# Eleven opening loads on another engine's queue: a two-layer hybrid trunk on one core

## The chip, the cores and the metric

The kernel runs on one core of one Trainium2 chip. The metric is the time of one execution on the device in microseconds (us); the median of three runs stands for a kernel. The engines are named as the profile names them: PE (TensorE, matrix products), DVE (VectorE), ACT (ScalarE), POOL (GpSimd) and SP (SyncE, which here does nothing but start DMA transfers). Each engine executes its own list of instructions in a fixed order, and waits on semaphores for the others.

## The reference

Two layers of a diffusion trunk work on 128 context rows and 1024 latent rows (1152 rows, nine tiles of 128), D_MODEL 1024, in float32. Each layer first computes a modulation from the condition vectors, which scales, shifts and gates everything behind it:

```python
def trunk_layer(x, cond, P, mixer):
    mod = jnp.einsum('bd,de->be', jax.nn.silu(cond), P['w_ada']) + P['b_ada']
    sh1, sc1, gt1, sh2, sc2, gt2 = jnp.split(mod[:, None, :], 6, axis=-1)
    h = rms_norm(x, P['g_pre_mix']) * (1.0 + sc1) + sh1
    o, extra = mixer(h)
    x = x + gt1 * rms_norm(o, P['g_post_mix'])
    h = rms_norm(x, P['g_pre_mlp']) * (1.0 + sc2) + sh2
    ...
```

The mixer projects h to four groups (latent attention, windowed attention, a gated delta-rule scan, a long convolution) and joins them; a squared-ReLU MLP follows. The filters of the long convolution come from a small network of sines over position features, which depends on neither x nor the condition:

```python
    h = jnp.sin(freq[0] * (feats @ P['hy_w1'].astype(F32) + P['hy_b1'].astype(F32)))
    h = jnp.sin(freq[1] * (h @ P['hy_w2'].astype(F32) + P['hy_b2'].astype(F32)))
```

## The kernel before

**What stands at the start.** The kernel first loads constants with `C` (line 198), all from SP: `condraw` (the condition vectors), `ident` (the identity matrix for transposes), `bada0` (the modulation's bias) and `g_pre_mix0`. ACT turns `condraw` into `cst` with a Silu (line 327); every product of the modulation reads `cst`. Two generators then run against one another. `hy_sines` (line 1496) computes the network of sines for both layers at once: it loads `feats` (17 rows of 1152 values) and six small pieces of the tile `hyw` (for each layer `w1` with 17 rows, `w2` with 64 rows, and `pp`; line 1508), runs three products `hy` of 17 rows, a run of DVE operations on the tile `hya`, a sine on ACT (line 1523), and the same again from `w2`. `lead` (line 2051) loads three tiles of x, runs the first part of the modulation, and loads the other six tiles.

**The modulation's first part.** `ada` (line 385) loads 32 tiles `wada` of 256 KB (line 392) and multiplies each into one accumulating tile, as four products side by side. The tiles rotate through two pools, named T (4 buffers) and L (8 buffers), so twelve can be under way; the thirteenth load waits for a product that has read its buffer. Afterwards ACT copies the sum to `adarow` (line 398), PE transposes it (`adat`), and ACT applies it to the transposed x (`h`, line 481), which becomes `hT`, the input of every product of the input projection (`pj`, weights `wa`, loaded by line 251 and split into `wah` and `wal`).

**What sets the order.** Lists of all engines are made ahead of time by a list scheduler that plays the program through with its own estimates of durations. An instruction that moves in the list at the start shifts the estimates of all that follow, and so the order of instructions far behind it may change too. Each transfer of SP or ACT also takes one of eight completion semaphores (DMAHW0 to DMAHW7), and does not start before the transfer that had the same semaphore last has landed.

**Later places that are named below.** The delta-rule scan of each layer needs an inverse, built on POOL (tiles N, written to DRAM and read back as `NaTG`) and finished by products `G` on PE. The scan itself is the products `u` and `dS` with the state `St`. `ht` and `tt` are transposes, and `hc` is a tile that they read. Later parts of the modulation load `wada` through the same line 392.

Of the kernel before, what the change touches and what calls it, by code (L numbers as in the profile page):

```python
# [34 lines left out]
def shape_constants():  # L35
# [21 lines left out]
    def rope_rows(dim):  # L57
        co, si = angles(dim)
        C = np.repeat(co, 2, 1).T
        S = np.repeat(si, 2, 1).T * np.where(np.arange(dim) % 2 == 0, -1.0, 1.0)[:, None]  # L60
        r = 128 // dim
        return np.tile(C, (r, 1)), np.tile(S, (r, 1))
# [4 lines left out]
    C = np.repeat(co, 2, 1)  # L67
    S = np.repeat(si, 2, 1) * np.where(np.arange(32) % 2 == 0, -1.0, 1.0)[None, :]
    c["rope_k"] = np.stack([C, S], 0).reshape(2, 8, 128, 32).transpose(2, 0, 1, 3).astype(f)

    def feats(L):
# [92 lines left out]
class Trunk:  # L164
# [30 lines left out]
    def S(self, shape, name, bufs=2, dt=F32, p=128):  # L195
        return self.psm.tile([p] + list(shape), dt, tag=name, name=self.nm(name), bufs=bufs)

    def C(self, shape, name, src=None):
        t = self.pc.tile([128] + list(shape), F32, tag=name, name=name)
        if src is not None:  # L200
            self.nc.sync.dma_start(out=t, in_=src)
        return t

    def dram(self, shape, name):
# [115 lines left out]
    def consts(self):  # L320

        I, nc = self.I, self.nc

        cond = self.C((8, 2), "condraw", I["cond"])
        self.cst = self.C((8, 32), "cst")
        nc.vector.memset(self.cst, 0.0)
        nc.scalar.activation(out=self.cst[:, :, 0:2], in_=cond, func=AF.Silu)
        self.ident = self.C((128,), "ident", I["ident"])
        self.mhalf = self.C((1,), "mhalf")
        nc.vector.memset(self.mhalf, -0.5)  # L330
        self.mod = [self.C((3, 8, 2, 2), f"mod{l}") for l in range(DEPTH)]
        self.AB = [self.C((2, 8, 2), f"ab{l}") for l in range(DEPTH)]
        self.gvec = {}
        self.bada = [self.C((48,), "bada0", I["b_ada"][0])]
        self.gvec["g_pre_mix", 0] = self.C((8,), "g_pre_mix0", I["g_pre_mix"][0])

    def scratch(self):

# [189 lines left out]
    def rope_rows(self, x, tab, c):  # L528

        nc = self.nc  # L530
        C, S, sh = (self.H(name=n) for n in ("rC", "rS", "rsh"))
        nc.sync.dma_start(out=C, in_=self.I[tab][0][:, c])
        nc.sync.dma_start(out=S, in_=self.I[tab][1][:, c])
        nc.vector.stream_shuffle(out=sh, in_=x[:, c], mask=[i ^ 1 for i in range(32)])
        nc.gpsimd.tensor_tensor(out=sh, in0=sh, in1=S, op=ALU.mult)
        nc.vector.tensor_tensor(out=x[:, c], in0=x[:, c], in1=C, op=ALU.mult)
        nc.vector.tensor_tensor(out=x[:, c], in0=x[:, c], in1=sh, op=ALU.add)
# [958 lines left out]
    def hy_sines(self, tag):  # L1496

        nc, I = self.nc, self.I
        V = nc.vector
        small = self.W(name="hyw", tag=tag)  # L1500
        w1, w2, pp = small[:, 0:128], small[:, 128:256], small[:, 256:260]
        V.memset(w2, 0.0)
        h = self.W(name="feats", tag=tag)
        nc.sync.dma_start(out=h[:17], in_=I["feats"])
        for l in range(DEPTH):
            q = slice(64 * l, 64 * l + 64)
            for dst, src in ((w1[:17, q], I["hy_w1"][l]), (w2[q, q], I["hy_w2"][l]), (pp[q], I["hy_pp"][l])):
                nc.sync.dma_start(out=dst, in_=src)
        for st, w in ((0, w1[:17]), (1, w2)):
            a = self.W(name="hya", tag=tag)  # L1510
            for c0, n in NCH:
                ps = self.P(name="hy")
                self.mm(ps[:, :n], w, h[:w.shape[0], c0:c0 + n])
                V.tensor_scalar(out=a[:, c0:c0 + n], in0=ps[:, :n], scalar1=pp[:, 2 * st:2 * st + 1],
                                scalar2=pp[:, 2 * st + 1:2 * st + 2], op0=ALU.add, op1=ALU.mult)
            k = self.W(name="hyk", tag=tag)
            M = 1.5 * 2 ** 23
            V.tensor_scalar(out=k, in0=a, scalar1=1.0 / (2 * math.pi), scalar2=M, op0=ALU.mult, op1=ALU.add)
            V.tensor_scalar(out=k, in0=k, scalar1=M, scalar2=None, op0=ALU.subtract)
            V.scalar_tensor_tensor(out=a, in0=k, scalar=-6.28125, in1=a, op0=ALU.mult, op1=ALU.add)  # L1520
            V.scalar_tensor_tensor(out=a, in0=k, scalar=-(2 * math.pi - 6.28125), in1=a, op0=ALU.mult, op1=ALU.add)
            V.tensor_scalar(out=a, in0=a, scalar1=3.1415925, scalar2=-3.1415925, op0=ALU.min, op1=ALU.max)
            nc.scalar.activation(out=a, in_=a, func=AF.Sin)
            h = a
            yield 5
        self.sines = h
# [714 lines left out]
```

## Time and profile before

| | us |
|---|---|
| median of three runs | 3825.18 |
| the three runs | 3819.07 to 3829.11 |
| the profiled execution | 3828.84 |
| its span in the trace | 3827.1 |
| PE busy in the span | 3531.1 (92%) |
| DVE busy | 2279.6 (60%) |
| ACT busy | 1355.6 (35%) |

The span is the time from the first to the last instruction of the trace; the remaining 1.7 us of the profiled execution lie around it. Shares are averages over the whole kernel; the stretches of it have different limits, so the windows and the waits are read beside them.

### The profile page before, as it was taken

What the parts mean: (1) busy time and instruction counts of PE and PEld (TensorE: products, weight loads), DVE (VectorE), ACT (ScalarE), POOL (GpSimd) and SP (SyncE); (2) the same over time, 40 slices, a digit from 0 to 9 for tenths busy, and PEclk for the clock granted to TensorE, in tenths of its full rate; (3) what the DMA queues carried; (4) which work ended last, traced back from release to release, by engine and by line L of the source; (5) the groups of instructions that cost most, each with busy time, mean ns of one, the idle gap of its engine ahead of it and who ended that gap; (6) DMA issues with size and microseconds to landing.
All of it is one profiled execution on the core that took longest, in us unless ns stands there. A gap on an engine that the chain in (4) does not pass through costs nothing. (4 is left out here: it accounts for less than half of the span.)

```text
span 3827.1 us, 57478 instructions
## 1 busy us (share of the span) xinstructions
PE 3531.1 (92%) x21710; PEld 2958.8 (77%) x21710; DVE 2279.6 (60%) x4583; ACT 1355.6 (35%) x2970; POOL 853.1 (22%) x806
## 2 busy tenths in 40 slices
PE   7989888899899999999989798787999999999998
PEld 4879764366689999999968797645666899999997
DVE  5765577696645444444586664768884544444446
ACT  5434343264542222122354234323564422222112
POOL 1151521264430000000131524213553200000003
PEclk9999889897899999999999898897889999999999
DMA  5356486831421111111234465756314211111113
GB/s 202 115 120 158 139 275 202 235 90 39 138 87 47 45 44 34 44 45 45 96 103 131 108 144 161 258 187 177 84 50 138 72 45 45 45 45 42 40 41 121
DMA packets 364672, 405.31 MB, mean 106 GB/s; under 512 B 115815, under 2 KB 237157, under 8 KB 364394
## 3 DMA queue, kind: packets, MB, share of 16 engines
q1 hardware_dynamic: 364394, 401.63, 34.9%
q8 instruction: 171, 2.80, 0.3%
q14 instruction: 107, 0.88, 0.1%
HBM read 298.34 MB, written 103.19 MB: 105 GB/s over the span
## 5 line engine op out<-in xcount | busy, mean ns | idle before, releaser
L213 PE MATMUL hid<-hT,w1h 128*128 128x384 f32 x3072 | 786.5, 335 | 0.1
L213 PE MATMUL pj<-hT,wah 128*128 128x384 f32 x2112 | 575.1, 351 | 9.0 <-ACT wah L253 4.2
L1831 DVE TENSOR_TENSOR acc<-acc,mo 128x512 f32<-128x512 f32 x504 | 346.1, 687 | 391.8 <-PE mo L213 391.8
L213 PEld LDWEIGHTS hid<-hT,w1h 128*128 128x128 f32 x3072 | 557.7, 188 | 14.4 <-ACT h L481 1.1
L213 PE MATMUL hid<-hT,w1l 128*128 128x384 f32 x1536 | 514.1, 335 | 0.0
L213 PE MATMUL mo<-w2h,ul 128*128 128x512 f32 x1116 | 435.0, 392 | 0.0
L213 PE MATMUL mo<-w2h,uh 128*128 128x512 f32 x1080 | 422.7, 391 | 0.0
L213 PE MATMUL mo<-w2l,uh 128*128 128x512 f32 x1080 | 422.7, 391 | 0.0
L213 PEld LDWEIGHTS pj<-hT,wah 128*128 128x128 f32 x2112 | 395.3, 196 | 21.9 <-issue 7.8
L662 POOL TENSOR_TENSOR e<-e,e 128x512 f32<-128x512 f32 (+1 forms) x216 | 307.3, 1424 | 313.8 <-DVE el L232 145.2
L269 POOL TENSOR_TENSOR postr<-postr,mhalf 128x1 f32<-128x1 f32 x36 | 22.3, 621 | 1568.9 <-DVE postr L268 1568.6
L213 PE MATMUL pj<-hT,wal 128*128 128x384 f32 x1056 | 367.5, 348 | 0.7 <-DVE wal L232 0.7
L242 ACT CAST w2h<-w 128x512 fp32r<-128x512 f32 x128 | 70.3, 619 | 732.9 <-PE mo L213 728.8
L213 PEld LDWEIGHTS hid<-hT,w1l 128*128 128x128 f32 x1536 | 288.3, 188 | 2.5
L232 DVE TENSOR_TENSOR el<-e,eh 128x512 fp32r<-128x512 f32 (+1 forms) x252 | 241.4, 977 | 25.1 <-ACT eh L653 20.4
L213 PEld LDWEIGHTS mo<-w2h,ul 128*128 128x128 f32 x1116 | 209.6, 188 | 46.1
L213 PEld LDWEIGHTS mo<-w2h,uh 128*128 128x128 f32 x1080 | 202.8, 188 | 37.5
L213 PEld LDWEIGHTS mo<-w2l,uh 128*128 128x128 f32 x1080 | 202.7, 188 | 36.5
L213 PEld LDWEIGHTS pj<-hT,wal 128*128 128x128 f32 x1056 | 206.3, 195 | 4.6 <-issue 2.0
L1814 DVE SCALAR_TENSOR_TENSOR relu<-hid,relu 128x384 f32<-128x384 f32 x180 | 99.5, 554 | 166.9 <-ACT relu L1813 166.9
L213 PE MATMUL ada<-wada,cst 128*32 128x512 f32 x384 | 130.8, 692 | 45.5 <-DMA wada<-in_w_ada 45.4
L232 DVE TENSOR_TENSOR wal<-wa,wah 128x512 fp32r<-128x512 f32 x88 | 67.6, 773 | 147.2 <-ACT wah L253 118.2
(502 smaller groups left out, 6366.6 us busy)
## 6 DMA issues: line engine op xcount, KB each, us to landing
w<-in_w SPq DMA_DIRECT2D x256, 256.0 KB
wada<-in_w_ada SPq DMA_DIRECT2D x192, 256.0 KB
wa<-in_wa SPq DMA_DIRECT2D x88, 256.0 KB
x<-xres SPq DMA_DIRECT2D x21, 512.0 KB
x<-in_x SPq DMA_DIRECT2D x18, 512.0 KB
Q<-rscr SPq DMA_DIRECT2D x32, 288.0 KB
o<-oscr SPq DMA_DIRECT2D x18, 512.0 KB
xres<-x SPq DMA_DIRECT2D x36, 256.0 KB
```

The lines of the kernel that those rows point to most:

```text
L213: self.last = self.nc.tensor.matmul(out, l, r, start=start, stop=stop, skip_group_check=True)
L232: self.nc.vector.tensor_tensor(out=lo, in0=x, in1=hi.bitcast(F32), op=ALU.subtract)
L242: self.nc.scalar.copy(out=hi[:, q], in_=st)
L269: self.nc.gpsimd.tensor_tensor(out=out, in0=out, in1=self.bcs(self.mhalf[:out.shape[0]], out.shape), op=ALU.pow)
L662: self.nc.gpsimd.tensor_tensor(out=acc, in0=acc, in1=e, op=ALU.add)
L1814: nc.vector.scalar_tensor_tensor(out=r[:, :n], in0=ps[:, :n], scalar=0.0, in1=r[:, :n], op0=ALU.max, op1=ALU.mult)
L1831: nc.vector.tensor_tensor(out=acc[t][:, ns], in0=acc[t][:, ns], in1=ps, op=ALU.add)
```

## The change

Four calls of `C` in `consts`, the load of `feats` and the six loads of `hyw` are started by ACT (`nc.scalar`) in place of SP. Nothing is computed differently.

```diff
-    def C(self, shape, name, src=None):
+    def C(self, shape, name, src=None, queue=None):
         t = self.pc.tile([128] + list(shape), F32, tag=name, name=name)
         if src is not None:
-            self.nc.sync.dma_start(out=t, in_=src)
+            (queue or self.nc.sync).dma_start(out=t, in_=src)
         return t
...
-        cond = self.C((8, 2), "condraw", I["cond"])
+        q = nc.scalar
+
+        cond = self.C((8, 2), "condraw", I["cond"], q)
...
-        self.ident = self.C((128,), "ident", I["ident"])
+        self.ident = self.C((128,), "ident", I["ident"], q)
...
-        self.bada = [self.C((48,), "bada0", I["b_ada"][0])]
-        self.gvec["g_pre_mix", 0] = self.C((8,), "g_pre_mix0", I["g_pre_mix"][0])
+        self.bada = [self.C((48,), "bada0", I["b_ada"][0], q)]
+        self.gvec["g_pre_mix", 0] = self.C((8,), "g_pre_mix0", I["g_pre_mix"][0], q)
...
-        nc.sync.dma_start(out=h[:17], in_=I["feats"])
+        nc.scalar.dma_start(out=h[:17], in_=I["feats"])
         for l in range(DEPTH):
             q = slice(64 * l, 64 * l + 64)
             for dst, src in ((w1[:17, q], I["hy_w1"][l]), (w2[q, q], I["hy_w2"][l]), (pp[q], I["hy_pp"][l])):
-                nc.sync.dma_start(out=dst, in_=src)
+                nc.scalar.dma_start(out=dst, in_=src)
```

SP's list before, behind the loads of `condraw`, `ident` and `bada`. A name in brackets is a semaphore for which the instruction waits; DMAHW4, in the row of `wada_180`, is the one that `feats` raises.

```order
L201 DMA g_pre_mix_108<-in_g_pre_mix 128x8
L1504 DMA feats_115<-in_feats 17x1152
L1508 DMA hyw_113<-in_hy_w 17x64
L1508 DMA hyw_113<-in_hy_w 64x64 [waits DVE_49]
L1508 DMA hyw_113<-in_hy_pp 64x4
L1508 DMA hyw_113<-in_hy_w 17x64 [waits DMAHW0_49]
L1508 DMA hyw_113<-in_hy_w 64x64 [waits DMAHW1_49]
L1508 DMA hyw_113<-in_hy_pp 64x4 [waits DMAHW2_49]
L392 DMA wada_177<-in_w_ada 128x512 [waits DMAHW3_49]
L392 DMA wada_180<-in_w_ada 128x512 [waits DMAHW4_49]
L392 DMA wada_183<-in_w_ada 128x512 [waits DMAHW5_49]
```

Seven more `wada` follow there, then three tiles of x, then 18 `wada`. SP's list after the change begins with twelve `wada`; these are the last two of them and what follows. DMAHW1 is raised in turn by `wada_177`, by `feats` and by the second `w1`, and DMAHW7 by `g_pre_mix` and then by the first `pp`.

```order
L393 DMA wada_224<-in_w_ada 128x512 [waits DMAHW4_49]
L393 DMA wada_230<-in_w_ada 128x512 [waits DMAHW6_49]
L1791 DMA x_140<-in_x 128x1024 [waits DMAHW7_49]
L1791 DMA x_152<-in_x 128x1024 [waits DMAHW0_49]
L1791 DMA x_164<-in_x 128x1024 [waits DMAHW1_49]
L393 DMA wada_227<-in_w_ada 128x512 [waits DMAHW2_49,PE_49]
L393 DMA wada_233<-in_w_ada 128x512 [waits DMAHW3_49,PE_49]
```

The eleven small loads are gone from SP, and `wada_227` is the first load that waits for PE (for five products: three `hy` and two `ada`); later the `wa_378` that stood ahead of `wada_287` stands behind the six loads of x. ACT's list, which opened with the table load and the Silu, now opens so:

```order
L201 DMA condraw<-in_cond 128x16
L201 DMA ident<-in_ident 128x128
L201 DMA bada_106<-in_b_ada 128x48
L328 ACT_TABLE_LOAD [waits DMAHW0_49]
L328 ACTIVATE cst<-condraw 128x8x2 [waits DVE_49]
L201 DMA g_pre_mix_108<-in_g_pre_mix 128x8
L1505 DMA feats_115<-in_feats 17x1152 [waits DMAHW1_49]
L1509 DMA hyw_113<-in_hy_w 17x64 [waits DMAHW3_49]
L1509 DMA hyw_113<-in_hy_w 64x64 [waits DMAHW5_49,DVE_49]
L1509 DMA hyw_113<-in_hy_pp 64x4 [waits DMAHW7_49]
L1509 DMA hyw_113<-in_hy_w 17x64 [waits DMAHW1_49]
L1509 DMA hyw_113<-in_hy_w 64x64 [waits DMAHW3_49]
```

Eight of the eleven loads now stand behind the Silu, and the second `w1` (17x64) waits on DMAHW1 until `feats` has landed. PE's list opens in both kernels with the three products `hy` that need `feats` and both `w1`; behind them come ten products `ada` before, thirteen after.

The scheduler also orders later stages anew; this is the second layer's inverse on PE, before, where the first `G` stands behind two of nine transposes of `hc`.

```order
L213 MATMUL pj_19970<-hT_11027,wal_19914 128x384
L229 MATMUL ht_3641_20144<-ident,hc_19588 128x128 x2
L213 MATMUL G_19719<-NaTG_19702,Q_19155 32x32
L213 MATMUL G_19757<-NaTG_19702,Q_19155 32x32
L229 MATMUL ht_3641_20144<-ident,hc_19588 128x128
```

The same place after the change:

```order
L213 MATMUL pj_19970<-hT_11027,wal_19914 128x384
L229 MATMUL ht_3641_20144<-ident,hc_19588 128x128 x4
L229 MATMUL ht_3643_20152<-ident,hc_19588 128x128 x4
L229 MATMUL ht_3645_20160<-ident,hc_19588 128x128
L213 MATMUL G_19719<-NaTG_19702,Q_19155 32x32
```

All nine transposes now stand ahead of the first `G`; and the two `G` that read `Q_19172`, which followed the transposes directly before the change, stand behind 40 products `pj` after it.

## Rows read from the trace of the kernel before

**Rows 1.** The page: engines' busy time, share of the span, instructions; the DMA queue.
```profile
PE 3531.1 (92%) x21710; PEld 2958.8 (77%) x21710; DVE 2279.6 (60%) x4583; ACT 1355.6 (35%) x2970; POOL 853.1 (22%) x806
q1 hardware_dynamic: 364394, 401.63, 34.9%
```
**Rows 2.** Windows: start:end us, length, busy of PE PEld DVE ACT POOL, PEclk, DMA share, GB/s.
```profile
8.00:10.00 2.00, 0.66 (x1) 0.50 (x2) 0.00 (x0) 0.00 (x0) 0.00 (x0) 1.00 0.51 141
10.00:12.00 2.00, 2.00 (x4) 1.00 (x3) 0.68 (x1) 0.00 (x0) 0.00 (x0) 1.00 0.98 346
30.00:38.00 8.00, 7.18 (x22) 1.11 (x20) 2.04 (x3) 2.03 (x3) 0.00 (x0) 1.00 1.06 389
40.00:60.00 20.00, 14.41 (x84) 11.82 (x85) 14.90 (x54) 19.76 (x47) 5.48 (x8) 0.96 0.76 264
80.00:180.00 100.00, 100.00 (x523) 86.48 (x522) 63.57 (x156) 50.03 (x93) 10.93 (x8) 1.00 0.32 112
2400.00:2600.00 200.00, 153.06 (x1396) 99.50 (x1392) 143.21 (x427) 60.42 (x200) 45.90 (x44) 0.86 0.72 235
```
**Rows 3.** Timeline of SP, 0 to 42 us: start, length, line, operation, how many.
```profile
0.74 0.39 SPq L201 DMA_DIRECT2D condraw<-in_cond  x1
...
2.60 0.33 SPq L1504 DMA_DIRECT2D feats<-in_feats  x1
...
6.24 6.38 SPq L392 DMA_DIRECT2D wada<-in_w_ada  x10
...
33.03 0.33 SPq L392 DMA_DIRECT2D wada<-in_w_ada  x1
```
**Rows 4.** What SP waited for in 0 to 14 us: total, times, longest.
```profile
SPq L392 <- DMA feats<-in_feats: 1.6, 1, 1.6
```
**Rows 5.** Timeline of SP, 8 to 10 us.
```profile
8.47 1.77 SPq L392 DMA_DIRECT2D wada<-in_w_ada  x4
```
**Rows 6.** Timeline of ACT, 0 to 42 us; in brackets the idle time before, and its end.
```profile
2.41 1.28 ACT L327 ACT_TABLE_LOAD   x1 [2.41 <-DMA condraw<-in_cond]
3.70 0.22 ACT L327 ACTIVATE cst<-condraw 128x16 f32<-128x16 f32 x1
...
37.64 0.62 ACT L253 CAST wah<-wa 128x512 fp32r<-128x512 f32 x1 [2.15 <-DMA wa<-in_wa]
```
**Rows 7.** Timeline of PE, 0 to 42 us.
```profile
9.34 4.20 PE L213 MATMUL hy<-feats,hyw 17*128 17x384 f32 x6 [9.34 <-DMA hyw<-in_hy_w]
13.47 5.86 PE L213 MATMUL ada<-wada,cst 128*32 128x512 f32 x20
38.26 1.04 PE L213 MATMUL ada<-wada,cst 128*32 128x512 f32 x2 [0.30 <-DMA wada<-in_w_ada]
```
**Rows 8.** Timeline of PE, 2163 to 2182 us (layer 1's inverse).
```profile
2175.34 0.41 PE L213 MATMUL G<-NaTG,Q 32*32 32x32 f32 x4 [8.57 <-DMA NaTG<-nscr]
...
2176.44 1.54 PE L229 MATMUL ht<-ident,hc 128*128 128x128 f32 x6
2180.49 0.39 PE L213 MATMUL G<-NaTG,Q 32*32 32x32 f32 x4 [2.51 <-DMA NaTG<-nscr]
```
**Rows 9.** The page: a group of products, count | busy us, mean ns | idle before.
```profile
L213 PE MATMUL pj<-hT,wah 128*128 128x384 f32 x2112 | 575.1, 351 | 9.0 <-ACT wah L253 4.2
```
**Rows 10.** What PE waited for, 1900 to 2800 us: total, times, longest.
```profile
PE ada L213 <- DMA wada<-in_w_ada: 27.9, 7, 14.5
...
PE u L213 <- DVE St L1368: 8.9, 4, 4.3
```
**Rows 11.** Timeline of POOL, 228 to 285 us (layer 0's inverse), two of its pieces.
```profile
238.59 0.55 POOL L1212 TENSOR_TENSOR N<-N,tmp 72x156 f32<-72x156 f32 x1
239.22 5.04 POOL L1210 TENSOR_TENSOR tmp<-N,U 72x175 f32<-72x175 f32 x1
```
**Rows 12.** What PE waited for, 180 to 720 us (layer 0's mixer).
```profile
PE G L213 <- DMA NaTG<-nscr: 18.3, 1, 18.3
```

## The prediction

> **What bounds the kernel now.** I read the page's shares first, then windows, then the waits of PE and of SP. PE is busy 92% of the span, the DMA queue 34.9% [rows 1]: over the whole kernel PE is the bound. The windows show where it is not [rows 2]. From 80 to 180 us PE is busy 100 of 100 us, and time saved ahead of such a stretch is kept, because PE simply starts it earlier. In the opening it is different. PE starts its first product at 9.34 us, when `hyw` has landed [rows 7]; from 10 us on the DMA engines are full (0.98, then 1.06 at 389 GB/s), while in 8 to 10 us they stand at 0.51 [rows 2]. The last product of the modulation's first part starts at 38.26 and waits for its own load [rows 7]. So the opening is a stream of loads, and what counts is when the stream starts and whether it has holes. From 40 to 60 us ACT is busy 19.76 of 20 us [rows 2]; it applies the modulation there and starts when the modulation is ready, so an earlier end of the stream passes through.
>
> The hole ahead of the stream has two parts. SP issues eleven small loads from 0.74 on and its first `wada` at 6.24 [rows 3]. Its next `wada` needs the semaphore that `feats` raises: SP waited 1.6 us for it [rows 4] and went on at 8.47 [rows 5]. `feats` was issued at 2.60 [rows 3], so from issue to landing it took 8.47 - 2.60 = 5.87 us.
>
> **SP's opening.** SP's first `wada` moves from 6.24 to about 0.74: 5.50 us. The `wa` that stood ahead of `wada_287` now stands behind the x loads: 256 KB at 389 GB/s [rows 2] is 0.67 us. If the stream had no hole, the last product would start 5.50 + 0.67 = 6.2 us sooner. That is one end. But only twelve buffers exist: the thirteenth load, `wada_227`, waits for the second product `ada`, which stands in PE's list behind the three products `hy`. So the stream stops after twelve `wada` and three x, and goes on when PE starts. What decides is when PE starts; I call that T0 (9.34 before).
>
> **ACT's opening and T0.** `condraw` is issued at 0.74 as before, and the table load starts at 2.41 when it lands: 1.67 us from issue to landing. Table load and Silu end at 3.70 + 0.22 = 3.92 [rows 6]. Before, nothing on ACT's list was waiting there; now eight loads stand behind it. `g_pre_mix` takes an issue of about 0.4 (0.39 [rows 3]), so `feats` is issued at 4.3 where it was 2.60. Landing 5.87 later: 10.2. The second `w1` waits for that landing by its semaphore, and needs at least the 1.67 of `condraw`: T0 = 11.9 at the earliest. At the other end `feats` no longer has the DMA engines nearly to itself, as it had before; twelve `wada` run beside it. If that doubles the part behind the fixed 1.67, that is 5.87 - 1.67 = 4.2 us more, T0 = 16.1. No row shows `feats` beside a full stream. I take the middle, T0 = 14.0, because DMA is full as soon as SP streams [rows 2], and the stream covers only part of the time of `feats`.
>
> The Trainium skill, "DMA: Bandwidth & Descriptors", section "Queues, rings and completion order", has each DMA engine take turns between its queues by packet, which speaks against the change: `feats` would share its engine with the weights. By that rule T0 lies nearer the late end. The sum does not use it.
>
> **From T0 to the last product.** The three `hy` take 4.2 us in this trace (six records from 9.34 to 13.54) and the first two `ada` together about 1.4 (1.06 for one, and 5.86/20 = 0.29 for a next, as four run at once) [rows 7]. So `wada_227` is issued at T0 + 5.6. Issue 0.4, 1.67 to landing, then 20 `wada` at 256 KB/389 GB/s = 0.67 and one `wb` of 192 KB at 0.5: T0 + 5.6 + 0.4 + 1.67 + 13.5 + 0.5 = T0 + 21.7. With T0 = 14.0 the last product starts at 35.7 instead of 38.26: **-2.6 us**, ends -4.7 (T0 = 11.9) and -0.5 (T0 = 16.1). The opening breaks even at T0 = 16.6. So PE's first product comes later than before, and the modulation ends sooner all the same.
>
> The sines on ACT (second product `hy`) hide beside the `ada` products; the x tiles are normalised there as well. If that cover is gone, each sine costs what ACT waits for DVE, but none stands on the chain to the last `ada`. The moved `wa` must be cast by ACT behind the modulation: 0.62 us [rows 6], in the stretch where ACT is full [rows 2]: **+0.6**, ends 0 and 0.7.
>
> **The order further on.** Most of the new order changes nothing where PE is full. Where PE waits it may. In layer 0 PE waits 18.3 us for the inverse [rows 12], whose inputs stand 3 to 13 products later in PE's list; at 575.1/2112 = 0.27 us a product [rows 9] that is 0.8 to 3.5 us later for POOL's chain, and the wait grows by it: **+0.8**, since the first input moves by three. That chain can also move by itself: one of POOL's pieces took 5.04 us where its neighbour took 0.55 [rows 11], so 4.5 us either way stay open.
>
> In layer 1 the first `G` waits 8.57 and the next pair 2.51 [rows 8]. Seven transposes move ahead of the first: 7 x 1.54/6 = 1.8 us of work into a wait. The pair that waited 2.51 now follows 40 `pj`, some 40 x 0.27 = 10.9 us, and waits no more. Together 4.3 us if nothing behind `G` gets late, 0 if the products behind `G` wait instead. I take the middle, **-2.1**. Behind it, in 2400 to 2600, PE is idle 200 - 153.06 = 46.9 us [rows 2], with single waits for `wada` of up to 14.5 us and for the scan's `St` of up to 4.3 [rows 10]; there the order differs in nearly every row, and I can give it a bound only, in the rivals.
>
> **Sum.** -2.6 + 0.6 + 0.8 - 2.1 = -3.3 us. On the profiled execution that is 3828.84 - 3.3 = 3825.5; that execution lies 3.66 above the median, so I forecast for the median 3825.18 - 3.3 = **3822**. About 0.3% (11.5 us) is what a measurement of this kernel tells from no change, so the forecast is "the same".
>
> **Rivals.**
> 1. *The whole gap is gained.* If `feats` is quick and the stream has no hole to speak of, the opening gives 6.2: 3825.2 - 6.2 + 0.6 + 0.8 - 2.1 = 3818. For it: DMA stands at 0.51 in 8 to 10 us [rows 2]. Against: `wada_227` stands behind PE's first products in any case. The Trainium skill, "DMA: Bandwidth & Descriptors", section "Issuing engines are not separate DMA queues", says that loads from several engines save only the time to start them. By that rule one would expect about the 5.50 us by which SP's first `wada` moves.
> 2. *The serial chain on ACT eats it.* `condraw`, table, `feats`, `w1` follow each other on one list, and PE's first product with all of the modulation stands behind the last of them. If T0 goes past 16.6 us the opening is later than before; at T0 = 20 by 3.4 us: 3825.2 + 3.4 + 0.6 + 0.8 - 2.1 = 3828.
> 3. *Layer 1 gains more than the opening.* The longest wait for `wada` there, 14.5 us [rows 10], goes, because the load comes sooner against the scan: 3821.9 - 14.5 = 3807. For it: the opening alone cannot pay this much, but 46.9 us of idle PE lie there. Against: these loads wait for buffers that earlier `ada` products free, and that is unchanged.
> 4. *Layer 1 loses, and the kernel is slower.* The last `pj` stands 68 rows sooner in PE's list (10703, was 10771) with about three steps of the scan left over. Those run with nothing between them; at the 4.3 us of the longest wait for `St` [rows 10] that is 12.9 us. With the opening's -2.6 + 0.6 + 0.8: 3825.2 + 12.9 - 1.2 = 3837. It decides from three steps on; with one step it is 3828.
>
> **How the numbers follow.** Forecast (net within 8 us of it, up to 3830) 0.46, rival 1 0.13, rival 2 0.10, rival 3 0.20, rival 4 0.11. Faster by over 0.3% needs under 3813.7: rival 3 and a third of rival 1, 0.24. Slower needs over 3836.7: most of rival 4 and a little of rival 2, 0.11. The same: 0.65. The range reaches below to rival 3's 3807 less a part of the POOL piece, 3805, and above to just short of rival 4, with 10 us over the median, 3835.
>
> **What would show it.** Right: SP's first `wada` at about 0.7; `feats` issued at 4.3 from ACT; PE's first product at 12 to 16 us, later than 9.34; an idle stretch of SP ahead of the thirteenth `wada`; the last `ada` of the first part at 33.6 to 37.8; the wait at layer 1's first `G` near 6.8 and the 2.51 gone. Wrong: the last `ada` after 38.3, or a difference of more than 10 us that lies behind 2000 us.

## The result, and the profile after

The change makes the kernel slower: 3852.86 us (median of four runs, 3848.59 to 3856.91) where the kernel before took 3824.92 (median of four, 3819.07 to 3829.11). The ratio is 1.0067, with a 95% interval of 1.0053 to 1.0080: about 28 us, outside the forecast range of 3805 to 3835. The profiled execution of the change took 3848.59 us, with a span of 3846.8; it is the fastest of the four, so the two traces differ by 19.7 us of span where the medians differ by 27.9. The other 8 us lie between executions of the same kernel, and no trace shows them.

The page first: busy times after. The eleven moved loads run on a DMA queue of their own (q10 on the page, 0.22 MB), which the page of before doesn't have.

```profile
PE 3538.8 (92%) x21710; PEld 2965.1 (77%) x21710; DVE 2269.5 (59%) x4583; ACT 1363.5 (35%) x2974; POOL 858.9 (22%) x806
```

Beside [rows 1], nothing tells where 20 us went: the work is the same, and PE is busy 7.7 us longer with the same 21710 instructions. The next thing to read is where in the program the two traces drift apart. I cut each at the same five events of PE's list: the end of the first modulation (`adat`), the first product of layer 0's MLP, the first transposes of its sum (`ht` of `acc`, shortly before its end), the first attention product `S` of layer 1, and the first product of layer 1's MLP. These are the windows of before from the MLP of layer 0 on (columns as in [rows 2]):

```profile
1124.10:1915.30 791.20, 791.18 (x4019) 720.55 (x4020) 394.31 (x647) 183.59 (x375) 25.48 (x25) 1.00 0.16 51
1915.30:2606.20 690.90, 580.83 (x5078) 485.85 (x5076) 456.87 (x1128) 279.47 (x676) 217.79 (x238) 0.89 0.54 160
2606.20:3011.60 405.40, 373.46 (x1690) 272.71 (x1688) 288.63 (x490) 211.24 (x430) 183.22 (x139) 0.89 0.35 99
```

And the same three stretches of the kernel after:

```profile
1129.20:1920.40 791.20, 791.18 (x4019) 720.55 (x4020) 394.10 (x647) 183.61 (x375) 25.75 (x25) 1.00 0.16 51
1920.40:2595.20 674.80, 572.74 (x5069) 480.62 (x5067) 438.99 (x1098) 280.15 (x675) 216.20 (x236) 0.91 0.54 159
2595.20:3031.30 436.10, 382.15 (x1699) 277.58 (x1696) 292.77 (x520) 215.02 (x434) 194.58 (x141) 0.86 0.35 100
```

Read by their second column, the lengths. Up to the MLP of layer 0 the change is 5.1 us behind (1129.2 for 1124.1). The MLP up to its transposes takes 791.20 us in both: PE is full there and nothing changes. From there to `S`, which is layer 1's mixer in the main, the change is **16.1 us shorter** (674.8 for 690.9), and the attention from `S` to the MLP is **30.7 us longer** (436.1 for 405.4). The three differences make 5.1 - 16.1 + 30.7 = 19.7, the whole difference of the spans. That is the result: a place that the change doesn't touch, 2600 us behind it, in which PE stands idle 54.0 us in place of 31.9 (length less PE's busy time) and has a mean granted clock of 0.86 of full speed in place of 0.89.

**The opening** did what it was built to do at its start. SP's timeline after, 0 to 46 us, beside [rows 3, 5], and then what SP waited for in that stretch (total, times, longest):

```profile
0.74 12.55 SPq L393 DMA_DIRECT2D wada<-in_w_ada  x12
...
20.78 10.64 SPq L393 DMA_DIRECT2D wada<-in_w_ada  x16
```

```profile
SPq L393 <- DMA wada<-in_w_ada: 8.6, 12, 2.6
SPq L393 <- PE ada L213: 7.0, 6, 5.3
```

ACT's timeline after, beside [rows 6]:

```profile
0.74 0.41 ACTq L201 DMA_DIRECT2D condraw<-in_cond  x1
...
4.24 1.28 ACT L328 ACT_TABLE_LOAD   x1 [4.24 <-DMA condraw<-in_cond]
...
4.69 0.53 ACTq L1505 DMA_DIRECT2D feats<-in_feats  x1
...
11.56 2.08 ACTq L1509 DMA_DIRECT2D hyw<-in_hy_w  x2
```

PE's timeline after, beside [rows 7]; and the row of before in which PE takes up the finished modulation, which [rows 7] stops short of:

```profile
14.66 4.20 PE L213 MATMUL hy<-feats,hyw 17*128 17x384 f32 x6 [14.66 <-DMA hyw<-in_hy_w]
...
39.80 1.05 PE L213 MATMUL ada<-wada,cst 128*32 128x512 f32 x2
41.52 0.65 PE L229 MATMUL adat<-ident,adarow 128*128 128x128 f32 x4 [0.68 <-ACT adarow L399]
```

```profile
39.98 0.66 PE L229 MATMUL adat<-ident,adarow 128*128 128x128 f32 x4 [0.68 <-ACT adarow L398]
```

SP's first `wada` goes out at 0.74 in place of 6.24, and still `adat` comes at 41.52 in place of 39.98. The windows show how the lead is lost; three of before, then the same three of after, last column GB/s:

```profile
0.00:8.00 8.00, 0.00 (x0) 0.00 (x0) 0.70 (x5) 1.50 (x2) 0.20 (x4) 1.00 0.17 36
8.00:28.00 20.00, 16.97 (x54) 5.66 (x54) 12.17 (x23) 6.93 (x16) 2.17 (x3) 1.00 0.96 341
28.00:40.00 12.00, 10.03 (x38) 1.98 (x35) 4.70 (x6) 3.24 (x6) 0.00 (x0) 1.00 1.05 392
```

```profile
0.00:8.00 8.00, 0.00 (x0) 0.00 (x0) 0.70 (x5) 1.50 (x2) 0.20 (x4) 1.00 0.73 229
8.00:28.00 20.00, 12.04 (x37) 4.00 (x38) 8.13 (x14) 5.80 (x13) 1.11 (x2) 1.00 0.75 241
28.00:40.00 12.00, 11.30 (x51) 2.95 (x50) 8.12 (x12) 2.99 (x6) 0.55 (x1) 1.00 1.00 363
```

In the first 8 us the change moves (229 - 36) x 8 = 1.54 MB more. In 8 to 28 us it moves (341 - 241) x 20 = 2.00 MB less, in 28 to 40 us (392 - 363) x 12 = 0.35 MB less. At 389 GB/s [rows 2] that is 4.0 us won, then 5.1 and 0.9 us lost: 2.0 us in arrears, and 1.5 us is what `adat` shows. The stream has a hole where twelve buffers are full and SP waits for PE (5.3 us ahead of 20.78). SP also waits 8.6 us, in twelve waits of up to 2.6, for earlier `wada` whose semaphore a transfer needs. It does so before as well, 6.4 us in 19 waits of up to 1.0, while the stream is full; how much of the loss these waits make isn't shown.

### The profile page after: what moved, and what is told of

It reads as the page before. It is cut to its first block, busy times and chain, and to the rows that moved or that the text cites. A ratio compares the mean times of both kernels' runs of the same rounds, so it can differ in the third digit from the quotient of the medians.

```text
span 3846.8 us, 57468 instructions
## 1 busy us (share of the span) xinstructions
PE 3538.8 (92%) x21710; PEld 2965.1 (77%) x21710; DVE 2269.5 (59%) x4583; ACT 1363.5 (35%) x2974; POOL 858.9 (22%) x806
## 5 line engine op out<-in xcount | busy, mean ns | idle before, releaser
L213 PEld LDWEIGHTS pj<-hT,wah 128*128 128x128 f32 x2112 | 397.1, 197 | 25.1 <-issue 5.6
L213 PE MATMUL ST<-Q,K 96*128 96x512 f32 (+3 forms) x456 | 144.6, 451 | 10.6 <-DMA Q<-mscr 10.6
```

The source lines that it names most:

```text
L213: self.last = self.nc.tensor.matmul(out, l, r, start=start, stop=stop, skip_group_check=True)
```

## The experiments

The diff changes one thing in the program and two in the lists: the opening, and the order of nearly everything behind it. To take them apart, the experiments build the program twice, with the eleven loads on SP (`False`) and on ACT (`True`), read the order of all instructions from both, compose an order from pieces of them, and build a third time with edges that bind each instruction to the one ahead of it on its own engine. Such an edge is made without a semaphore (`NoSync`): it fixes the order of an engine's list and adds no wait of its own.

```diff
+        for n in order:
+            if n in known:
+                i = known[n]
+                if i.engine in last:
+                    tc.add_manual_dep(i, last[i.engine], mybir.DependencyInfo(
+                        mybir.DependencyClass.NoSync, mybir.DependencyReason.DATA), reason="order")
+                last[i.engine] = n
...
+    for act, mark in SEGMENTS:
+        o, marks = orders[act]
+        o = o[:o.index(marks[mark]) + 1] if mark else o
+        o = [n for n in o if n not in seen]
+        order += o
+        seen.update(o)
```

`SEGMENTS` says whose order holds up to which mark. The marks are `ada00` (the copy to `adarow` that ends the first modulation), `mlp07` (the middle of layer 0's MLP) and `ada12` (the copy that ends layer 1's last part of the modulation, just ahead of its `S`). Ratios are to the kernel before on the same chip, with 95% intervals.

### The opening or the order

Only the opening is the change's; behind `ada00` every engine goes on in the order of before.

```diff
+ACT_QUEUE = True
+SEGMENTS = [(True, 'ada00'), (False, None)]
```

> The change with its eleven loads on ACT and its own order up to the copy adarow of the modulation's first part; behind that point every engine's list is held to the order of the kernel before. Theory 'order' (what slowed the kernel is the new order of later stages, the opening itself gains the 3 us that the trace of after shows at layer 0's first inverse, 280.2 against 284.2 us): 3821 to 3823 us, ratio 0.999 to 1.000. Theory 'opening' (the loads on ACT cost it, by the late first product at 14.66 us or by transfers that shift): near the change, 3850 us, ratio 1.006 to 1.008.

Measured: 3832.76 us against 3827.96, ratio 1.0007 (0.9990 to 1.0024).

The reverse: loads on SP as before, the change's order behind `ada00`.

```diff
+ACT_QUEUE = False
+SEGMENTS = [(False, 'ada00'), (True, None)]
```

> The kernel before with all its loads on SP and its own order up to the copy adarow; behind that point every engine's list is held to the order of the change. Theory 'order': 3852 to 3858 us, ratio 1.007 to 1.009, with the losses at the same places as in the change (layer 0's attention about +7 us, layer 1 from its attention on about +30 us after a gain of some 11). Theory 'opening': 3825 us, ratio 1.000.

Measured: 3849.57 us, ratio 1.0048 (1.0033 to 1.0064). Theory 'order' missed its times in both, too low by some 10 us in the first and too high by 2 to 8 in the second, but both intervals exclude theory 'opening'. The loss goes with the order and not with the loads. The opening by itself, the thing that the change is about, is worth nothing that these runs can tell from zero, and the order that came along costs the rest.

### Which part of the order

The change's order through layer 0, that of before from the middle of its MLP; and the change's opening, before's order through layer 0, and the change's order from there.

```diff
+SEGMENTS = [(True, 'mlp07'), (False, None)]
```

> The change with its own order up to the middle of layer 0's MLP, behind it the order of the kernel before. Theory 'order' with the loss split as the two profiled executions show it (5.1 us at the first layer's MLP, the other 15 to 20 in layer 1): 3829 to 3833 us, ratio 1.001 to 1.002. If all of the loss came from layer 0's order: 3850 us. Theory 'opening': 3850 us.

```diff
+SEGMENTS = [(True, 'ada00'), (False, 'mlp07'), (True, None)]
```

> The change's opening, the order of the kernel before up to the middle of layer 0's MLP, behind it the order of the change. Theory 'order' with the split of the two profiled executions: 3836 to 3846 us, ratio 1.003 to 1.0055, with the loss between layer 1's attention and its MLP. If layer 0's order were the cause: 3822 us. Theory 'opening': 3850 us.

Measured: 1.0004 (0.9989 to 1.0018) for layer 0's order, 1.0060 (1.0037 to 1.0084) for layer 1's. All of the loss that can be told from zero lies in layer 1's order. The next three cut layer 1 at its `S`: the change up to there and before's order behind it; the change's order in layer 1's mixer alone; and the change's order from `S` on alone (the last two with the loads on SP).

```diff
+SEGMENTS = [((True, True), 'ada12'), ((False, False), None)]
```

> The change with its own order up to the copy adarow of layer 1's last modulation part (just ahead of layer 1's first attention product), behind it the order of the kernel before. Theory 'attention' (the loss lies in the order behind that point; S to the MLP took 436 us in the change and 405 before): about 3853 - 30 + part of the work that the change had put behind that point, 3822 to 3832 us, ratio 0.999 to 1.001. Theory 'backlog' (the change reaches that point 11 us sooner only because it leaves work behind, and pays whatever order follows): 3840 to 3850 us, ratio 1.004 to 1.0065.

```diff
+SEGMENTS = [((False, False), 'mlp07'), ((True, True), 'ada12'), ((False, False), None)]
```

> All loads on SP and the order of the kernel before, but from the middle of layer 0's MLP to the copy adarow of layer 1's last modulation part the order of the change. The change reaches that point 11 us sooner than before although it was 5 us late at the MLP. If that lead is worth something: 3808 to 3818 us, ratio 0.9955 to 0.998, faster than both kernels. By 'backlog': 3825 to 3835 us.

```diff
+SEGMENTS = [((False, False), 'ada12'), ((True, True), None)]
```

> All loads on SP and the order of the kernel before up to the copy adarow of layer 1's last modulation part, behind it the order of the change. Theory 'attention': the loss appears without anything else of the change, 3840 to 3855 us, ratio 1.004 to 1.0075, with PE waiting some 10 us for the row that is read back from mscr. Theory 'backlog': 3825 to 3832 us, ratio 1.000 to 1.0015.

Measured: 1.0023 (1.0006 to 1.0040), 1.0032 (1.0021 to 1.0044) and 1.0067 (1.0053 to 1.0081). The attention's order alone costs as much as the whole change. The mixer's order alone costs too, about 12 us, more than either of its theories allowed, although the mixer is what got shorter in the change; the parts don't add up to the whole. The stage lengths, read from the first products in each trace (`e7`, `e9` and `o1` to `o3` come below), show why the mixer's gain is lost:

| order of mixer, of attention | kernels | first product of layer 0's MLP to `S` | `S` to layer 1's MLP | both together |
|---|---|---|---|---|
| before, before | before, e1, e3, e9, o1 to o3 | 1475.5 to 1484.1 | 397.8 to 405.4 | 1874.2 to 1888.6 |
| change, change | after, e2, e4 | 1461.3 to 1466.0 | 434.2 to 436.1 | 1896.4 to 1902.1 |
| change, change but for two transfers | e7 | 1463.2 | 422.9 | 1886.1 |
| change, before | e5, e6 | 1482.7, 1487.2 | 398.0, 400.3 | 1880.7, 1887.4 |
| before, change | e8 | 1482.9 | 423.4 | 1906.3 |

The profiled execution of before is among the long ones of its row (1887.5), so the 16.1 and 30.7 us above hold for these two traces alone. And the table doesn't show where `e5` and `e6` lose their 9 and 12 us: their traces are no longer in these two stages than those with before's order. That stays open.

The change's order gains 10 to 23 us ahead of `S` only when its own attention follows, since there `S` starts before the tail of the scan and the transposes `oT` of its results are done. In before's attention nine `oT` stand ahead of `S` and wait for that tail. This is what PE waited for around that place in the kernel with the change up to `S` and before's order behind it (`e5`, 2550 to 3045 us):

```profile
PE oT L229 <- DVE gsk L276: 18.6, 1, 18.6
...
PE ada L213 <- DMA wada<-in_w_ada: 7.7, 4, 3.1
```

And this in the kernel before, same stretch:

```profile
PE ada L213 <- DMA wada<-in_w_ada: 21.1, 2, 14.5
```

The wait for `wada` of [rows 10], which rival 3 hoped to win, falls from 21.1 to 7.7 us; 18.6 us of waiting for the scan stand in its place. The scan is what ends there, whichever wait PE shows.

One more kernel tests that directly. It keeps before's order and moves only the last eight `wada` of layer 1 forward in SP's list so that PE needn't wait for them.

```diff
+ACT_QUEUE = (False, False)
+SEGMENTS = [((False, False), None)]
+MOVES = [('I-24531', 'I-24497'), ('I-24534', 'I-24531'), ('I-24537', 'I-24534'), ('I-24540', 'I-24537'),
+         ('I-24557', 'I-24503'), ('I-24560', 'I-24557'), ('I-24563', 'I-24560'), ('I-24566', 'I-24563')]
```

> The kernel before in its own order, with the last eight wada of layer 1 moved forward in SP's list: four ahead of the stores to goscr behind which they were issued at 2582 us, though the products that free their buffers were done by 2575.5; four directly behind the load VA. If SP's order makes PE's waits of 14.5 and 6.6 us there and the scan's last outputs can follow: adat some 8 to 14 us sooner, 3813 to 3820 us, ratio 0.9965 to 0.9985. By 'backlog' (the scan's last outputs are late in any order: 18.6 us of wait at oT once the wada are there): the wait moves to oT, 3824 to 3830 us, ratio 0.9995 to 1.001.

Measured: 3827.85 us against 3828.97, ratio 0.9994 (0.9978 to 1.0010). Its waits of PE, 2550 to 3000 us:

```profile
PE ada L213 <- DMA wada<-in_w_ada: 11.0, 3, 8.3
PE oT L229 <- DVE gsk L276: 7.1, 1, 7.1
```

The wait for `wada` falls from 21.1 to 11.0 and 7.1 us come up at `oT`, a wait that before doesn't have; the time doesn't move. (It also shows that an order bound by such edges costs nothing that can be measured, since apart from eight loads this is the kernel before.)

### What the attention loses

PE's waits in the change from `S` to the MLP (2590 to 3035 us), those that grew:

```profile
PE ST L213 <- DMA Q<-mscr: 10.6, 1, 10.6
...
PE op L213 <- ACT oh L1763: 6.1, 2, 4.7
...
PE rb L213 <- DVE rden L701: 4.8, 2, 3.0
...
PE oT L229 <- DVE o L1423: 3.3, 1, 3.3
```

The first is the largest, and before it was this:

```profile
PE ST L213 <- DMA Q<-mscr: 2.4, 1, 2.4
```

`ST` is the second pass of the scores, whose operand has one more row, the row of maxima. ACT writes that row (`mrow`), SP stores it to DRAM (`mscr<-mrow`) and loads it into the operand (`Q<-mscr`). The change's timeline of ACT and then of SP there:

```profile
2615.98 0.25 ACT L728 CAST mrow<-mT 8x128 fp32r<-8x128 f32 x1
```

```profile
2616.68 0.22 SPq L753 DMA_DIRECT2D K<-krowd  x1
2618.73 0.22 SPq L754 DMA_DIRECT2D Q<-krowd  x1
...
2620.60 1.48 SPq L2030 DMA_DIRECT2D oscr<-osk  x3
...
2625.36 0.34 SPq L729 DMA_DIRECT2D mscr<-mrow  x1
...
2627.41 1.05 SPq L775 DMA_DIRECT2D Q<-mscr  x1
```

The row is ready at 2616.2 and is stored at 2625.36: 9.1 us in which it stands in SP's one list behind seven loads, five of them left out above, and six stores `oscr`. For some 2.3 us of that SP waits for the semaphores of the loads `gzl`, which belong to the scan's tail; the rest is the issue, one after another, of what stands ahead of the row. But SP was late by then. From the first `S` to that store it waited 10.5 us in all for the scan's tail: 3.6 for the outputs `sc` and their stores, 2.7 for the load of these, 4.2 for `gzl`. Three of these waits:

```profile
SPq L749 <- DMA o<-goscr: 2.7, 1, 2.7
SPq L753 <- DMA gzl<-zscr: 2.4, 1, 2.4
...
SPq L754 <- DMA gzl<-zscr: 1.8, 1, 1.8
```

This is what the change's order carries past `S`: it issues the two `gzl` at 2607.87, 12.7 us behind the first `S`, where before issues them at 2587.39, 19 us ahead of it, and in before SP waits 0.4 us for the scan's tail between `S` and the row. The six stores `oscr<-osk` are no part of that. They hold results of the long convolution (line 2030, from the transposes `hoT`), and they stand right ahead of the row in before as well, where the row is nevertheless stored 0.5 us after it is ready. The test moves two transfers in SP's list: the store to directly behind `K<-krowd`, the load to directly behind `Q<-kscr`. (The eight semaphores, which are handed out in turn, shift with them.)

```diff
+ACT_QUEUE = (True, True)
+SEGMENTS = [((True, True), None)]
+MOVES = [('I-24739', 'I-24753'), ('I-24740', 'I-24756')]
```

> The change in its own order, with two transfers of SP in layer 1's attention moved ahead of the loads and stores that they stood behind: the write of the row mrow to mscr and its reading into Q (the copy to mrow ended at 2616.2 us, the write was issued at 2625.4). If SP's order there makes PE's wait of 10.6 us: the wait falls to 2 or 3 us and the kernel to about 3845 us, 8 us under the change, ratio 1.0045 to 1.006. If something else is late behind it (the exponentials, the scan's last outputs): 3850 to 3855 us, as the change.

Measured: 3841.58 us against 3827.49, ratio 1.0034 (1.0020 to 1.0049). The rest of the order is the change's own, so about half of its loss, 1.0067 - 1.0034 or some 12 us, is gone; that is more than the 8 us expected, and each ratio is known to about 0.0015, or 6 us. SP's two rows in this kernel, PE's first `ST`, and its window from `S` to the MLP:

```profile
2617.89 0.27 SPq L729 DMA_DIRECT2D mscr<-mrow  x1
...
2620.35 0.38 SPq L775 DMA_DIRECT2D Q<-mscr  x1
```

```profile
2622.94 4.71 PE L213 MATMUL ST<-Q,K 97*128 97x512 f32 x12 [1.03 <-DMA Q<-mscr]
```

```profile
2595.80:3018.70 422.90, 380.04 (x1699) 275.54 (x1697) 295.50 (x520) 214.94 (x434) 193.90 (x141) 0.87 0.36 103
```

The row is stored 7.5 us sooner, the wait at `ST` falls from 10.6 to 1.0, and the stretch takes 422.9 us in place of 436.1. What is left of the loss against before is spread over the shorter waits above and a granted clock of 0.87 where before has 0.89; PE is busy 380.04 us there for 373.46. These I haven't separated further: they stay open.

`e8` shows what the row on SP's list does not explain. Its loads `gzl` are issued 19 us ahead of `S`, as in before, SP waits for nothing of the scan's tail behind `S`, and the row is stored 1.8 us after it is ready. PE waits 8.9 us for it all the same. ACT's row, SP's, and PE's:

```profile
2631.18 0.25 ACT L728 CAST mrow<-mT 8x128 fp32r<-8x128 f32 x1
```

```profile
2633.24 0.34 SPq L729 DMA_DIRECT2D mscr<-mrow  x1
```

```profile
2640.07 5.46 PE L213 MATMUL ST<-Q,K 97*128 97x512 f32 x12 [8.86 <-DMA Q<-mscr]
```

Between the transpose of the row (`mT`) and `ST` PE's list has only nine `oT` in the change's order, 1.2 us of work here; before has ten more products `S` there, from 2630.09 to 2634.1 us. And `e8`'s stretch from `S` on, 423.4 us, is as long as that of `e7`, 422.9. So, with one trace of each, the loss behind `S` is of two kinds: some 13 us (436.1 less 422.9) for the row on an SP list that the scan's tail has held up, and 18 to 25 us (423.4 less the 398 to 405 of before's order) for the rest of the attention's order. That the second is lost by what stands between `mT` and `ST`, and at places like it, is argued from these rows and not tested.

### The opening, taken apart

Three kernels with before's order behind `ada00`: only the four constants on ACT; only `feats` and `hyw` on ACT; and all eleven on ACT, with `feats`, both `w1` and both `pp` moved to directly behind `condraw` in its list.

```diff
+ACT_QUEUE = (True, False)
+SEGMENTS = [((True, False), 'ada00'), ((False, False), None)]
```

> One part of the change: only condraw, ident, bada and g_pre_mix on ACT; feats and hyw stay on SP ahead of wada; behind the copy adarow the order of the kernel before. Theory 'chain' (in the change PE's first product is late because feats stands behind the Silu on ACT and the second w1 behind feats): feats is issued near 0.8 to 1.3 us, PE starts at 7.5 to 8.5 us and the transposes adat at 38 to 38.8 us, a little under the 39.98 of before. If the late start came from the four constants on ACT: PE starts after 12 us. In total within the noise, 3820 to 3830 us.

```diff
+ACT_QUEUE = (False, True)
+SEGMENTS = [((False, True), 'ada00'), ((False, False), None)]
```

> The other part alone: only feats and hyw on ACT, the four constants stay on SP ahead of wada; behind the copy adarow the order of the kernel before. Theory 'chain' (the wait for feats' landing on one list, and its share of the DMA engines with a full stream of wada): feats is issued at 1.2 us already, so PE starts at 8.5 to 11 us, and adat at 37 to 40 us. If sharing with the stream alone makes feats slow whatever its issue: 12 us or more, adat 41 us or more. In total within the noise, 3820 to 3830 us.

```diff
+ACT_QUEUE = (True, True)
+SEGMENTS = [((True, True), 'ada00'), ((False, False), None)]
+MOVES = [('I-122', 'I-96'), ('I-119', 'I-96'), ('I-120', 'I-96'), ('I-117', 'I-96'), ('I-116', 'I-96')]
```

> The change's opening (SP opens with wada, all eleven loads on ACT), with feats, both w1 and both pp on ACT right behind condraw; behind the copy adarow the order of the kernel before. By the sum of the prediction with T0 = 8 to 10 us the last ada starts at T0 + 21.7 = 30 to 32, bounded by the stream at 32, and adat at 34: 5 to 6 us under before, 3817 to 3823 us. If the way from T0 to the last ada is longer than the sum has it (in the change it took 25.1 instead of 21.7): adat at 36 to 38 us.

Measured: 1.0005 (0.9990 to 1.0020), 1.0013 (0.9997 to 1.0030) and 1.0007 (0.9990 to 1.0024). Their first product and their `adat`, in this order:

```profile
8.00 4.20 PE L213 MATMUL hy<-feats,hyw 17*128 17x384 f32 x6 [8.00 <-DMA hyw<-in_hy_w]
...
40.91 0.66 PE L229 MATMUL adat<-ident,adarow 128*128 128x128 f32 x4 [0.68 <-ACT adarow L399]
```

```profile
9.33 4.17 PE L213 MATMUL hy<-feats,hyw 17*128 17x384 f32 x6 [9.33 <-DMA hyw<-in_hy_w]
...
38.72 0.66 PE L229 MATMUL adat<-ident,adarow 128*128 128x128 f32 x4 [0.68 <-ACT adarow L399]
```

```profile
10.92 4.17 PE L213 MATMUL hy<-feats,hyw 17*128 17x384 f32 x6 [10.92 <-DMA hyw<-in_hy_pp]
...
41.11 0.66 PE L229 MATMUL adat<-ident,adarow 128*128 128x128 f32 x4 [0.68 <-ACT adarow L399]
```

PE's first product comes at 8.0, 9.3, 10.9 and (in the change) 14.7 us, and `adat` at 40.9, 38.7, 41.1 and 41.5. `adat` was expected at 38.0 to 38.8 in the first and at 34, or 36 to 38, in the third; both came later. So neither an earlier first product nor an earlier start of SP's `wada` brought an earlier end of the modulation by itself. One trace of each is too little to order them: six traces that share the change's opening (the change, e1, e3, e4, e5 and e7) have `adat` at 41.0 to 45.9, and five that open as before (before, e2, e6, e8 and e9) have it at 39.5 to 40.3. That all six lie later than all five is the firmest reading: the change's opening ends later than before's by 1 to 6 us, not earlier. None of the versions tried beats the kernel before by more than the measurement can tell.

## Why the prediction was wrong

**The opening's first half was right.** SP's first `wada` at 0.74, PE's first product later than before at 14.66 (said: 14.0, between 11.9 and 16.1), an idle SP ahead of the thirteenth `wada`. Inside, two errors cancelled. `condraw` landed 4.24 - 0.74 = 3.50 us after its issue and not 1.67, since it now ran beside four `wada`; but the loads behind it didn't wait for table load and Silu, as I had it: `g_pre_mix` was issued at 4.31, while the table load ran. So `feats` was issued at 4.69 (said: 4.3). It landed 11.56 - 4.69 = 6.87 us later (said: 5.87, up to 10.1), and the second `w1` 14.66 - 11.56 = 3.10 after its issue (said: at least 1.67).

The Trainium skill, "DMA: Bandwidth & Descriptors", section "Queues, rings and completion order", lets the queues of an engine take turns by packet. These three landing times agree with that in direction: 3.50 for 1.67, 6.87 for 5.87, 3.10 for 1.67.

**The step "T0 + 21.7" failed.** It lets the stream run from the thirteenth load on at 389 GB/s without a hole. SP's thirteenth load went out at 20.78, as it should (T0 + 5.6 = 20.3). But it did not run full from there on: it moved 186 GB/s in 20 to 24 us, 262 in 24 to 28, and was full only from 28 us. The last product of the first part started at 39.80, which is T0 + 25.1 and not T0 + 21.7; so the sign for being wrong, a last `ada` after 38.3, was met. (The sum also reads 1.06 us for one `ada` where its row in [rows 7] has 1.04; nothing hangs on it.) `adat`, which follows the last product, came 1.5 us later than before; the sum had 2.6 us sooner, and three of the five other traces with this opening put it later still. Rival 1, the whole gap gained, falls with it, and so does the condition of rival 2: the first product did stay below 16.6, and the opening was later all the same.

**The terms +0.6 and +0.8** can't be told from scatter. The first MLP product came 5.1 us later in the change, but among five traces with the same opening and, but for one, the same order of layer 0 as before it ranges from 1124.1 to 1131.9. The wait for layer 0's inverse fell rather than grew, against [rows 12]:

```profile
PE G L213 <- DMA NaTG<-nscr: 16.4, 1, 16.4
```

My step, inputs that stand a few products later and so a longer wait, had the wrong sign: the wait ended at 280.2 us where it ended at 284.2 before. Either way it didn't matter, as the run with layer 0's order alone shows (1.0004).

**The term -2.1 failed in its place.** The first `G` of layer 1 waited 18.9 us where I had 6.8, that is the 8.57 of [rows 8] less 1.8:

```profile
2181.59 0.78 PE L213 MATMUL G<-NaTG,Q 32*32 32x32 f32 x8 [18.91 <-DMA NaTG<-nscr]
```

The 2.51 are gone as said. Work moved ahead of a wait shortens it only if its end stays where it is; here the inverse ended 6.25 us later (2181.59 for 2175.34), 5.1 of them because all of layer 1 starts later, and PE came to it 4.1 us sooner (2181.59 - 18.91 = 2162.7, before 2175.34 - 8.57 = 2166.8). A wait is the distance between two arrivals, and I had moved one of them only. What the longer wait cost by itself no run shows.

**What decided stood in no term, and this is the step that failed.** The prediction says of 2400 to 2600 us that the order "differs in nearly every row" and that it can give a bound only, in the rivals; the sum puts the order there, and everything behind it, at nothing. Measured, the order alone costs 1.0048, or 21.6 us between the medians, and the attention's order alone 1.0067. Both bounds saw something. Rival 3's wait for `wada` did shrink, and the change came to `S` 16.1 us sooner; but the scan ends no sooner for it. Rival 4 had the right sign, but its cause was at most a part. It priced three steps of the scan at 12.9 us where they stand. What the runs show instead is paid behind the scan, in the attention: some 13 us where the row that PE needs stands on an SP list that the scan's tail has held up, and more, 18 to 25 us, in `e8`, where SP waits for nothing of the scan behind `S`. No row of mine shows SP's list in the attention, and [rows 10] has PE's waits alone. The marker for being wrong, "more than 10 us that lies behind 2000 us", was the right one.

**The chances** followed: with "the same" at 0.65 I had taken the order behind the opening for a small term with its mean near zero. The measured span of such orders is 1.0004 to 1.0067, and the opening itself is 1.0007.

## What to carry to other kernels

Where a scheduler plays the program through, an edit at its start is two edits: the one in the diff, and a new order everywhere behind it. Pin the order and time them apart before believing either; here the edit was worth 0.07% (not to be told from zero) and the order that came with it 0.5 to 0.7%. When an order changes, look for small transfers on the way to PE, and read what stands ahead of them in SP's one list, since loads that wait there, and stores that could go later, hold up one that is needed now; and before counting an engine's wait as a gain, ask which wait comes next.

## What the runs showed of the hardware

- Small loads beside the stream of large ones were slow to land: `condraw` (128 x 16 values) took 3.50 us beside four `wada` where it took 1.67 beside other small loads; `feats` 6.87 where it took 5.87; a `w1` of 17 x 64 values 3.10 us.
- ACT issued DMAs while work that stands ahead of them in its list was still to come: `g_pre_mix` went out at 4.31 us, 0.07 us after a table load of 1.28 us began, and `feats` at 4.69, while the Silu ahead of both started at 5.54.
- Busy DMA engines don't always move as much. For each unit of busy share, the change moved 229/0.73 = 314 GB/s in its first 8 us and 241/0.75 = 321 in 8 to 28, where before moved 341/0.96 = 355 in 8 to 28 and 392/1.05 = 373 in 28 to 40. Before's first 8 us, with little but small loads, moved 36/0.17 = 212. The runs don't show whether the small loads, which run beside the large ones in the change, are the reason.
